# Gather, running sum and product: 64 gather slots in place of 16, at most 8 gathers on their way, a new order of sums and products

## The chip, the cores and the metric

The kernel runs on one core of a Trainium2 chip. The metric is the device time of one execution in microseconds (us); where runs are timed, it is the median of several. A run counts as slow when it takes over 1.5% more than the fastest run of the same kernel. The time of an execution is 1.7 to 1.8 us longer than the span of its profile, so spans are compared with spans and times with times.

## The reference

```python
B, S, N, D = (16, 4096, 2048, 512)
gathered = x[b_idx, indices, :].copy()   # 2048 sorted rows of 4096, for each of 16 batches
cs = np.cumsum(gathered, axis=1)         # running sum over the rows
return np.matmul(cs, w)                  # w is 512 x 512, all fp32
```

The kernel cuts this into 256 tiles of 128 rows. A tile's gather reads 128 rows of 2,048 bytes from HBM, the chip's memory, and writes them as fp16; a tile's result is 128 rows of 2,048 bytes in fp32.

## The kernel before

Five engines and the queue of stores work as a pipeline. They wait for each other on semaphores, which are counters (`need`, `then_inc`). A slot is the buffer that takes the gathered rows of one tile. **POOL** issues one indirect DMA a tile, which gathers the rows and casts them on the way:

```python
def gather(t):
    g, r = divmod(t, R)                       # R = 2 tiles make a pair
    pool.need(s_a, R * (g + 1) - NG)          # PE has summed the tile that had this slot (NG = 16)
    ...                                       # which column of indices
    nc.gpsimd.indirect_dma_start(
        out=g16[g % (NG // R)][:, r, :], ...
    ).then_inc(s_g[t % NG], 16)
```

**PE** multiplies the tile by a triangle of ones, which gives running sums inside the tile, already transposed (`sums`); **DVE** adds the last column of the tile before (`carry`); PE multiplies by `w` (`project`); **ACT** copies the product to an output buffer; SP stores four tiles (1 MB) at a time:

```python
def sums(t, u, first=None):
    pe.need(s_g[t % NG], 16 * (t // NG + 1), tiles)     # gather t has landed
    ...                                                 # four matmuls, 128 x 128 each
def project(u, t, first=None):
    ...
    pe.need(s_d, ...)                                   # DVE has done the carry
    ...                                                 # four matmuls, 128 x 512 each
```

PE runs its instructions in order, and the order is fixed beforehand: sums run some tiles ahead of products.

```python
for u in range(T):
    lead = min(LEAD, 1 + (u + 2) // 4, 1 + (T - 1 - u) // 6)    # LEAD = 4
    first = u if u // R in PLAIN else u // R * R + R - 1
    while done < T and done <= max(first, u + lead):
        order.append((True, done))       # sums of tile `done`
        done += 1
    order.append((False, u))             # product of tile u
```

## Time and profile before

Before the prediction the kernel took 354.54 us (median of 3 runs, 354.28 to 355.03). The execution that was profiled was a slower one: it took 355.99 us, with a span of 354.3 us.

Three periods compete in the middle of the run: POOL's for issuing a gather, PE's for computing a tile, and that of the DMA engines for moving one. Ask which is the longest; the prediction works them out, and shows the lines. None of the engines' shares alone says so: PE is counted busy for 86% of the span, 304.4 us, which is 25 us more than 256 tiles take where nothing holds it.

### The profile page before, as it was taken

The page shows a single profiled execution, that of the slowest core. Times are in us where ns is not written, and L with a number is a line of the kernel's source. Part 1 is how long each engine was busy: PE and PEld are TensorE (multiplying, and loading weights), DVE is VectorE, ACT ScalarE, POOL GpSimd, SP SyncE. Part 2 cuts the span into 40 slices and gives each one's busy share as a digit, 9 for nine tenths or more (in the row PEclk, how much of TensorE's full clock was granted, in tenths as well). Part 3 has the DMA queues.
Part 4 walks back from the last instruction along what each step waited for, and adds up shares of the span by engine and source line. Part 5 has one row for each costly group of instructions (what it writes and reads, how often), then busy time and mean ns, then how long its engine had stood idle before and what let it go on. Part 6 is the DMA issues. An engine that isn't in the chain of part 4 may idle for free.

```text
span 354.3 us, 6077 instructions
## 1 busy us (share of the span) xinstructions
PE 304.4 (86%) x2066; PEld 152.7 (43%) x2066; DVE 179.2 (51%) x263; ACT 152.4 (43%) x260; POOL 241.9 (68%) x266
## 2 busy tenths in 40 slices
PE   7787969889888898988889898888989889899993
PEld 2343525444444453444444344444445444444441
DVE  2563635545555554555555455455545546455441
ACT  2242525434444443443444344453444444344542
POOL 6777777777777777777777777776776767676000
PEclk9998989999999999999999999999999999999998
DMA  7999999999999999999999999999999999999995
GB/s 190 170 221 256 256 297 262 304 296 283 320 290 298 311 297 298 303 309 282 306 315 285 301 306 303 286 319 301 285 312 300 301 296 306 302 290 317 301 328 228
DMA packets 56010, 102.12 MB, mean 288 GB/s; under 512 B 5824, under 2 KB 38848, under 8 KB 56000
## 3 DMA queue, kind: packets, MB, share of 16 engines
q0 software_dynamic: 36864, 33.57, 58.9%
q1 hardware_dynamic: 18576, 67.90, 50.0%
q10 hardware_dynamic: 560, 0.53, 0.6%
q8 instruction: 5, 0.08, 0.1%
q14 instruction: 5, 0.04, 0.0%
HBM read 68.42 MB, written 67.11 MB: 383 GB/s over the span
## 4 chain that ended last, share of the span: by engine, by line
DMA 58%; POOL 20%; PE 12%; issue 8%; POOLq 0%; ACT 0%; SPq 0%
DMA g<-in_x_dram,idxg 58%; POOL g L120 20%; PE pb L183 9%; PE pa L139 4%; DMA idx_first<-in_indices_dram 1%; POOLq L279 0%; ACT ob L195 0%; SPq L403 0%; SPq L88 0%
## 5 line engine op out<-in xcount | busy, mean ns | idle before, releaser
L120 POOL DMA_INDIRECT g<-in_x_dram,idxg x252 | 236.4, 938 | 82.2 <-issue 64.2
L183 PE MATMUL pb<-w,cst 128*128 128x512 f16 x1024 | 264.8, 382 | 1.4 <-DVE cst L171 1.0
L171 DVE TENSOR_TENSOR cst<-pa,cst 128x512 f16<-128x512 f32 x240 | 166.1, 692 | 152.9 <-PE pa L139 151.5
L195 ACT COPY ob<-pb 128x512 f32<-128x512 f32 x256 | 149.8, 585 | 191.8 <-PE pb L183 191.8
L139 PE MATMUL pa<-ut,g 128*128 128x128 f16 x1008 | 99.5, 222 | 40.7 <-DMA g<-in_x_dram,idxg 39.5
L139 PEld LDWEIGHTS pa<-ut,g 128*128 128x128 f16 x1008 | 70.1, 98 | 124.0 <-DMA g<-in_x_dram,idxg 90.9
L183 PEld LDWEIGHTS pb<-w,cst 128*128 128x128 f16 x1024 | 89.9, 98 | 64.6 <-issue 2.5
L158 DVE CAST cst<-pa 128x512 f16<-128x512 f32 x16 | 11.1, 692 | 9.4 <-PE pa L139 9.4
L285 PE MATMUL pb<-zeros 128*128 128x512 f16 x16 | 5.7, 519 | 1.5 <-DVE zeros L289 1.5
L120 POOL DMA_INDIRECT g<-in_x_dram,idx_first x4 | 3.9, 986 | 1.6 <-issue 0.9
L285 PEld LDWEIGHTS pb<-zeros 128*128 128x128 f16 x16 | 1.9, 125 | 4.0 <-issue 2.0
L292 DVE CAST idxf<-idx 128x128 f32<-128x128 uint32 x2 | 0.5, 227 | 4.5 <-DMA idx<-in_indices_dram 4.5
L358 ACT ACT_TABLE_LOAD x1 | 1.3, 1283 | 2.5 <-issue 2.5
L361 ACT CAST w<-w 128x512 f16<-128x512 f32 x2 | 1.1, 614 | 2.8 <-DMA w<-in_w_dram 2.8
L139 PE MATMUL pa<-uq,g 128*128 128x128 f16 x16 | 1.6, 220 | 0.2
L139 PEld LDWEIGHTS pa<-uq,g 128*128 128x128 f16 x16 | 1.0, 97 | 1.6 <-DMA g<-in_x_dram,idxg 0.6
L297 PE MATMUL pb<-ident,idxf 128*128 128x128 f32 x2 | 0.7, 374 | 0.7 <-DVE idxf L292 0.7
L297 PEld LDWEIGHTS pb<-ident,idxf 128*128 128x128 f32 x2 | 0.4, 183 | 1.6 <-DVE idxf L292 1.3
L306 DVE CAST w<-w 128x512 f16<-128x512 f32 x2 | 0.8, 445 | 0.4 <-DMA w<-in_w_dram 0.4
L289 DVE MEMSET zeros<- 128x256 uint32 x1 | 0.3, 272 | 1.1 <-SPq L88 1.1
L303 DVE CAST idxg<-pb 128x128 uint32<-128x128 f32 x2 | 0.6, 288 | 0.2 <-PE pb L297 0.2
L245 POOL MEMSET ident<- 128x128 f32 x1 | 0.2, 204 | 0.5 <-SPq L88 0.5
(10 smaller groups left out, 1.9 us busy)
## 6 DMA issues: line engine op xcount, KB each, us to landing
out_dram<-ob SPq DMA_DIRECT2D x62, 1024.0 KB, 8.0
g<-in_x_dram,idxg POOLq DMA_INDIRECT x252, 15.7
out_dram<-ob SPq DMA_DIRECT2D x4, 256.0 KB, 3.2
out_dram<-ob SPq DMA_DIRECT2D x2, 512.0 KB, 4.2
w<-in_w_dram ACTq DMA_DIRECT2D x2, 256.0 KB, 3.9
w<-in_w_dram SPq DMA_DIRECT2D x2, 256.0 KB, 4.4
idx<-in_indices_dram SPq DMA_DIRECT2D x2, 128.0 KB, 3.1
g<-in_x_dram,idx_first POOLq DMA_INDIRECT x4, 4.0
```

The lines of the kernel that those rows point to most:

```text
L120: nc.gpsimd.indirect_dma_start(out=g16[g % (NG // R)][:, r, :], out_offset=None, in_=x_flat, in_offset=bass.IndirectOffsetOnAxis(ap=ap, ax ...
L139: mm = nc.tensor.matmul(out=pa[t % NA][:, c], lhsT=g16[g % (NG // R)][:, r, c * P : (c + 1) * P], rhs=uq[:] if first is None and g in PLAI ...
L158: nc.vector.tensor_copy(out=dst, in_=src).then_inc(s_d, 1)
L171: nc.vector.tensor_tensor(out=dst, in0=src, in1=last, op=mybir.AluOpType.add).then_inc(s_d, 1)
L183: mm = nc.tensor.matmul(out=pb[u % NB][:], lhsT=cst[g % NC][:, c, j, :], rhs=w16[:, c, :], start=(c == 0), stop=(c == DC - 1),)
L195: nc.scalar.copy(out=ob[g // W % NO][:, g % W, j], in_=pb[u % NB][:]).then_inc(s_e, 1)
L285: nc.tensor.matmul(out=pb[NB - 1][:], lhsT=zeros[:, :P], rhs=zeros[:], start=True, stop=True)
L297: nc.tensor.transpose(out=pb[k % NB][:, :P], in_=idxf[:, k, :], identity=ident[:]).then_inc(s_pt, 1)
L303: nc.vector.tensor_copy(out=idxg[:, k, :], in_=pb[k % NB][:, :P]).then_inc(s_prep, 1)
L306: nc.vector.tensor_copy(out=w16[:, c, :], in_=w32[:, c, :]).then_inc(s_wc, 1)
L358: nc.scalar.copy(out=spare[:], in_=zeros[:, :1])
L361: nc.scalar.copy(out=w16[:, c, :], in_=w32[:, c, :]).then_inc(s_wc, 1)
```

## The change

The intent is to uncouple the gathers from PE (64 slots), to keep the DMA queue short (8 on their way), and to start products sooner at the beginning and sums sooner at the end. The core of the diff:

```diff
-    NG = 16
+    NG = 64
+    FLY = 8
+    NS = 32
+    FREE = 8
...
+    V = NG
...
-        pool.need(s_a, R * (g + 1) - NG)
+        if t % FREE == 0:
+            pool.need(s_a, t + FREE - NG)
+        if t >= FLY:
+            pool.need(s_g[(t - FLY) % NS], 16 * ((t - FLY) // NS + 1))
...
-        lead = min(LEAD, 1 + (u + 2) // 4, 1 + (T - 1 - u) // 6)
+        lead = min(LEAD, 1 if u < 2 else 2 + (u + 4) // 12, (T - 1 - u) // 2)
...
-    step = 2 * U
+    step = 2 * V
...
-    with nc.tensor.Fori(2 * U // R, (T - 2 * U) // R, U // R) as first:
+    with nc.tensor.Fori(2 * U // R, (T - 2 * U) // R, V // R) as first:
```

The rest counts semaphores relative to the loop's start, since a round of PE's loop now has 64 tiles.

More of the change, by code (lines that the diff above doesn't have):

```diff
@@ L62 @@
     U = NT
-    assert U % NG == 0 and U % (W * R * NO) == 0 and U % NA == 0 and U % (R * NC) == 0 and U % NB == 0
+    V = NG
+    assert V % NS == 0 and NS == 16 * R and 2 * U % NS == 0 and (T - 4 * U) % V == 0 and U % (W * R * NO) == 0 and U % NA == 0 and U % (R * NC) == 0 and U % NB == 0
     assert D == 512 and N % (R * P) == 0 and T % P == 0
@@ L99 @@
     s_ol = sem("s_ol")
-    s_g = [sem(f"s_g{i}") for i in range(NG)]
+    s_g = [sem(f"s_g{i}") for i in range(NS)]
     s_o = [sem(f"s_o{i}") for i in range(NO)]
@@ L125, in gather @@
             element_offset=(t // NT) * S * D,
-        ).then_inc(s_g[t % NG], 16)
+        ).then_inc(s_g[t % NS], 16)
     PLAIN = (0, G - 1)
@@ L133, in sums @@
         tiles = None if first is None else R * first
-        pe.need(s_g[t % NG], 16 * (t // NG + 1), tiles)
-        pe.need(s_d, t - NA + 1, tiles)
+        skip = 0 if first is None else 2 * U
+        pe.need(s_g[t % NS], 16 * (t // NS + 1) - skip // R, first)
+        pe.need(s_d, t - NA + 1 - skip, tiles)
         for c in range(DC):
             if c == 1 and u is not None:
-                pe.need(s_e, u - NB + 1, tiles)
+                pe.need(s_e, u - NB + 1 - skip, tiles)
             mm = nc.tensor.matmul(
@@ L141, in sums @@
                 lhsT=g16[g % (NG // R)][:, r, c * P : (c + 1) * P],
-                rhs=uq[:] if first is None and g in PLAIN else ut[:],
+                rhs=uq[:] if g in PLAIN else ut[:],
                 start=(c == 0),
@@ L177, in project @@
         tiles = None if first is None else R * first
-        pe.need(s_e, u - NB + 1, tiles)
-        pe.need(s_d, u + 1 if first is None and g in PLAIN else R * (g + 1), tiles)
+        skip = 0 if first is None else 2 * U
+        pe.need(s_e, u - NB + 1 - skip, tiles)
+        pe.need(s_d, (u + 1 if g in PLAIN else R * (g + 1)) - skip, tiles)
         for c in range(DC):
             if c == 2 and t is not None:
-                pe.need(s_d, t - NA + 1, tiles)
+                pe.need(s_d, t - NA + 1 - skip, tiles)
             mm = nc.tensor.matmul(
@@ L330 @@
     tail = order.index((False, T - 2 * U - 1)) + 1
-    step = 2 * U
+    step = 2 * V
     for i in range(head + step, tail):
-        assert order[i] == (order[i - step][0], order[i - step][1] + U)
+        assert order[i] == (order[i - step][0], order[i - step][1] + V)
     def run(i, first=None):
@@ L337, in run @@
         after = next((v for k, v in order[i + 1 :] if k != is_sums), None)
-        if first is not None:
-            t -= 2 * U
-            after -= 2 * U
         if is_sums:
```

## The prediction

> **What bounds the kernel now.** I read the page first, then the DMA view for single stretches, then the chain of work that ended last and POOL's waits.
>
> From the page of the kernel before:
>
> ```profile
> PE 304.4 (86%) x2066; PEld 152.7 (43%) x2066; DVE 179.2 (51%) x263; ACT 152.4 (43%) x260; POOL 241.9 (68%) x266
> ...
> q0 software_dynamic: 36864, 33.57, 58.9%
> q1 hardware_dynamic: 18576, 67.90, 50.0%
> ...
> L120 POOL DMA_INDIRECT g<-in_x_dram,idxg x252 | 236.4, 938 | 82.2 <-issue 64.2
> ...
> g<-in_x_dram,idxg POOLq DMA_INDIRECT x252, 15.7
> ```
>
> Queue 0 carries the gathers (counted as the fp16 bytes that are written), queue 1 mostly the stores. Their packets together take 109% of what 16 engines have: some overlap, and little room. PE's 86% is no proof of a PE bound: where nothing holds it, the timeline shows a tile every 1.09 us (sums at 22.46 and 23.55 us), which is 279 us for 256 tiles, and PE's waits show 39.5 us for gathers. POOL could be the bound: between two gathers lie 938 ns of work and 0.30 us of "issue", 1.24 us a tile, 318 us in all.
>
> The DMA view of the long middle (75 to 325 us), of a microsecond with gathers alone (307 to 308), and of two with stores alone (345 to 347) decide it:
>
> ```profile
> DMA packets 40650, 75.01 MB, mean 300 GB/s; under 512 B 3850, under 2 KB 28509, under 8 KB 40648
> ...
> DMA packets 228, 0.20 MB, mean 203 GB/s; under 512 B 30, under 2 KB 228, under 8 KB 228
> ...
> DMA packets 208, 0.82 MB, mean 408 GB/s; under 512 B 6, under 2 KB 10, under 8 KB 208
> ```
>
> A tile's gather writes 128 x 512 fp16 = 131,072 bytes: at 203 GB/s, 0.646 us. A tile's store is 262,144 bytes: at 408 GB/s, 0.643 us. One after the other that is 1.29 us, and the middle really needs 393,216 bytes / 300 GB/s = **1.31 us a tile**. So the two simply share the 16 engines in time, and the engines have no free time from 75 us on. 1.31 is above POOL's 1.24 and PE's 1.09. 256 tiles x 1.31 = 335 us; the span is 354.3. The other 19 us are engine time lost at the two ends. Of the first 25 us, gathers (2.08 MB at 203 GB/s) use 10.2 and queue 1 (1.88 MB) and the weights' queue (0.53 MB) at 408 GB/s use 5.9, so 9 are lost; from 25 to 50 us (2.34 and 4.45 MB) 2.6 are lost; from 340 us to the end (0.07 and 3.76 MB) 4.8.
>
> The end, in the chain from 320 us, and POOL's waits from 200 to 320 us:
>
> ```profile
> 325.73 20.86 DMA g<-in_x_dram,idxg
> 346.59 0.05 issue
> 346.63 0.40 PE pa L139 x4
> 347.03 0.86 PE pb L183 x4
> 347.89 0.01 issue
> 347.90 1.04 PE pb L183 x4
> 348.94 0.02 issue
> 348.96 0.59 ACT ob L195
> ...
> POOL g L120 <- issue: 21.8, 71, 0.5
> POOL g L120 <- PE pa L139: 11.9, 22, 1.1
> ```
>
> The last gather is issued at 325.7 and lands 20.9 us later. Counting gathers between issue and landing in the trace gives 2 on their way in the first 20 us, 7 at 60 to 80 us, 15 from 200 us on. POOL runs at 1.24 us against 1.31 for the engines, so the queue grows until 16 slots are full at about 200 us; from then POOL waits for PE. This wait is a symptom: it costs nothing, because gathers lie ready on the engines all the time.
>
> Each gather is counted in by 16 engines. In the trace's semaphore records 13 of the 16 arrive within about 2 to 4 us, and the last three up to 6 to 9 us after the first (gather 255: first 338.1, median 339.4, last 346.6 us). So a few engines are slower, and the slowest sets when a tile is there.
>
> **What the Trainium skill says.** "DMA: Bandwidth & Descriptors", section "Issuing engines are not separate DMA queues": DMAs started from any engine end on the same 16 and interleave. The trace agrees: 1.29 us worked out against 1.31 measured. The same page, "Where 436 GB/s comes from", puts the ports' ceiling at 435 GB/s; stores alone reached 408, and gathers alone 203 written, which is 406 read since each element shrinks from four bytes to two. So both run close to that ceiling, and a rearrangement of waits has some 7% to win at the very most. The same page, "Latency and other measured facts", says that engines 7 and 15 are usually slower, with a guess that the rings of software descriptors are the cause; the trace has a few late engines in every gather, but does not name them.
>
> **The change part by part.**
>
> 1. *64 slots.* They let gathers run up to 64 tiles ahead of PE. They can be filled only if tiles land faster than PE eats them. Tiles land every 1.31 us, PE needs 1.09: they stay empty. What they remove is POOL's wait for PE, 18.0 us in the whole run, which covered a full queue. Worth 0 us on the end.
>
> 2. *At most 8 on their way.* This is the part that binds. From some 60 us on POOL will wait for the gather eight before. Does the queue of the slowest engine ever run dry? When gather t-8 has landed, seven remain: 7 x 1.31 = 9.2 us of work; the new one needs 1.24 us for POOL and, from the first gathers (issued until 4.31, landed at 8.07), 3.8 us to land. 9.2 covers 5.0. The kernel before moved 291 GB/s at 60 to 80 us, with 7 on their way, against 300 in the middle, and part of those 3% is the mix there. So 0 to +3 us. Against that, fast engines can no longer run 7 us (5 tiles) ahead of the slow ones. If the slow ones are slow because the fast ones crowd them, this evens them out: the median engine finished the last gather 7 us before the slowest, so perhaps -4 us; if they are slow by themselves, 0. I give the first one chance in three: -1.3 us. Landing time should fall to about 8 x 1.31 = 10.5 us less POOL's own time, from 15.7; that shortens no path, as the engines stay full.
>
> 3. *More waits on POOL.* One on a gather's semaphore per gather, one on PE per 8 (before: one on PE per pair). Before, gathers with and without a wait had the same 1.24 us period, so a wait already met hides under the 938 ns. 0 us.
>
> 4. *Order at the start.* Writing both orders out: sums lead by 2 and 3 where they led by 3 and 4, up to tile 19. Stores begin about one tile earlier where the engines are underused: one tile's store is 0.64 us. -0.7 us.
>
> 5. *Order at the end.* The lead stays 4 until tile 247, then falls to 0; only product 255 is left behind the last sums, where two were. In the chain that removes 0.86 us of PE, but the carry on DVE (0.69 us) then stands open in front of the product, and products 247 and 251 come one sums later. -0.1 us, with a spread of 1.
>
> 6. *PE loop of 64 tiles in place of 16.* Three rounds in place of twelve. PE stood 2.5 us in "issue" before products, and it has 0.2 us a tile to catch up in. 0 us.
>
> Sum: 354.5 + 1 - 1.3 - 0.7 - 0.1 = 353.4; I lean slightly lower, as a shallower queue may also disturb the stores less, and take **352.5 us**.
>
> **The rivals.** *A: the cap takes the place of the slots and starves the engines.* For it: the late engines use up most of the eight, so that fast ones hold only 2 or 3, and gathers alone drain at 0.65 us while POOL supplies one in 1.24. Against: the slow engine sets the end, and has seven. If it bites, a tile goes to 1.34 or 1.36 us: 362 to 367 us. *B: the cap evens out the engines.* For it: the spread of 6 to 9 us appears only as the queue grows (about 1.5 us in the first 40 us). Against: it could grow simply because slow engines fall behind. Time 348 to 350 us. *C: POOL becomes the bound*, each wait costing 0.1 us: 1.34 us a tile, 360 us. Against it: the equal periods above. *D: products are held up by late gathers, and 64 slots cure it.* PE does wait, but for data, not for slots; then nothing is gained.
>
> **Range and chances.** The engines' 335 us stay. What moves is inside the 19 us at the ends, and I see at most 5 of them won. Low 347.5 (B with the gain at the start), high 358 (a mild A). Faster than 2% means below 347.5: 0.11. Slower than 2% means above 361.6, A or C in full: 0.07. Within: 0.82.
>
> **What would show each step.** Right: the middle still at about 300 GB/s; landing time about 9 us; POOL's waits for PE gone and in their place waits for gathers, from 60 us on; a last gather issued some 10 us later (about 336 us) and landing at 344 to 347; PE still waiting for gathers. A shows as the middle below 295 GB/s; B as 16 arrivals closer together and the last landing before 343; C as a POOL period over 1.3 us in the first 40 us. I am wrong if the engines move more than 305 GB/s in the middle: then queue depth itself cost throughput, and nothing in this trace says so.

## The result, and the profile after

The changed kernel took **354.76 us** (median of 4 runs, 354.56 to 355.15) beside 354.78 us of the kernel before. Ratios here are the mean time of one kernel's fast runs over that of the other's of the same rounds, so not quite the ratio of the medians; this one is 1.0001, with a 95% interval of 0.9983 to 1.0019. A second set of runs gave 1.0000 (0.9980 to 1.0021). The forecast of 2 us less did not come.

The page of the changed kernel, in the lines that answer to those of before:

```profile
PE 302.0 (85%) x2066; PEld 151.1 (43%) x2066; DVE 179.3 (51%) x263; ACT 152.4 (43%) x260; POOL 242.0 (68%) x266
...
q0 software_dynamic: 36864, 33.57, 59.2%
q1 hardware_dynamic: 18576, 67.90, 49.7%
...
L127 POOL DMA_INDIRECT g<-in_x_dram,idxg x252 | 236.5, 939 | 89.9 <-issue 55.1
...
g<-in_x_dram,idxg POOLq DMA_INDIRECT x252, 9.3
```

One number moved: the median gather lands 9.3 us after its issue in place of 15.7. Everything that costs time stayed. A shorter stay in a queue is no shorter run, when the server behind the queue is as busy as before. That it is, the DMA view of 75 to 325 us shows:

```profile
DMA packets 40624, 75.36 MB, mean 301 GB/s; under 512 B 3836, under 2 KB 28379, under 8 KB 40619
```

301 GB/s where it was 300: 393,216 bytes / 301 = 1.31 us a tile, as before. POOL's waits in the whole run (total us, times, longest):

```profile
POOL g L127 <- issue: 56.0, 177, 1.4
POOL g L127 <- DMA g<-in_x_dram,idxg: 29.9, 62, 1.1
POOL g L127 <- PE pa L147: 4.9, 16, 0.3
```

The wait for PE fell from 18.0 us (42 times) to 4.9, and a wait for gathers of 29.9 us took its place. Each of these times holds the 0.30 us that lie between any two gathers, so 16 waits that make 4.9 us are no wait at all. Without this gap there were some 5 us of waiting before (18.0 - 42 x 0.30) and some 11 us now (29.9 - 62 x 0.30). POOL has time to spare; a run below takes these waits away, and the time stays.

The chain of work that ended last, from 335 us:

```profile
328.59 9.62 DMA g<-in_x_dram,idxg
338.21 0.05 issue
338.26 0.40 PE pa L147 x4
338.66 1.73 PE pb L192 x8
340.38 0.22 PE pa L147 x4
340.61 1.73 PE pb L192 x8
...
346.58 0.24 PE pa L147 x4
346.82 0.02 issue
346.84 0.70 DVE cst L179
347.55 0.05 issue
347.59 1.05 PE pb L192 x4
348.64 0.02 issue
348.67 0.58 ACT ob L204
```

Here is what looks like a gain and is none. The last gather now lands at 343.4 us (344.1 in the second profile) and not at 346.6. But PE no longer waits for it: from 338.26 us on it does nine products, some of them held behind sums until then, and five sums, with one gap of 0.77 us for the last carry on DVE. Its last product ends at 348.64 where it was 348.94. From the last landing to the end of the span there are now 10.0 us (10.6 in the second profile); before there were 7.7.

### The profile page after: what moved, and what is told of

Same layout as the page of the kernel before. It is cut to its first block, busy times and chain, and to the rows that moved or that the text cites. A ratio compares the mean times of both kernels' runs of the same rounds, so it can differ in the third digit from the quotient of the medians.

```text
span 353.4 us, 6043 instructions
## 1 busy us (share of the span) xinstructions
PE 302.0 (85%) x2066; PEld 151.1 (43%) x2066; DVE 179.3 (51%) x263; ACT 152.4 (43%) x260; POOL 242.0 (68%) x266
## 4 chain that ended last, share of the span: by engine, by line
DMA 54%; POOL 27%; issue 10%; PE 6%; DVE 0%; ACT 0%; POOLq 0%; SPq 0%
DMA g<-in_x_dram,idxg 54%; POOL g L127 27%; PE pb L192 5%; PE pa L147 2%; DMA idx_first<-in_indices_dram 1%; DVE cst L179 0%; ACT ob L204 0%; POOLq L26 0%; SPq L409 0%; SPq L92 0%
## 5 line engine op out<-in xcount | busy, mean ns | idle before, releaser
L147 PE MATMUL pa<-ut,g 128*128 128x128 f16 x1008 | 98.5, 220 | 42.5 <-DMA g<-in_x_dram,idxg 41.6
L147 PEld LDWEIGHTS pa<-ut,g 128*128 128x128 f16 x1008 | 68.9, 98 | 126.0 <-DMA g<-in_x_dram,idxg 92.9
```

The costliest lines, as they stand in the source:

```text
L147: mm = nc.tensor.matmul(out=pa[t % NA][:, c], lhsT=g16[g % (NG // R)][:, r, c * P : (c + 1) * P], rhs=uq[:] if g in PLAIN else ut[:], star ...
```

## The experiments

The first explanation (theory 1) was that the cap had really won 3 us at the last landing, and that the new order at the end gave them back. Four kernels take the change apart.

**The cap alone**, on the kernel before:

```diff
+    FLY = 8
...
+        if t >= FLY:
+            pool.need(s_g[(t - FLY) % NG], 16 * ((t - FLY) // NG + 1))
```

> The kernel before with one thing added: a gather waits until the one eight before it has landed (16 slots, order and PE loop as before). Theory 1 (the cap wins some 3 us at the last landing, and the new order at the end gives them back): 352 to 353.3 us, last landing near 343, at least 1.3 us faster than before. Theory 2 (the cap is neutral on the landing path, the earlier landing of the profiled run is chance): 354.3 to 355.2 us, last landing near 346.

Measured: 355.35 us, ratio 1.0020 (1.0002 to 1.0039). The last landing is at 345.8 us, the landing time:

```profile
g<-in_x_dram,idxg POOLq DMA_INDIRECT x252, 9.0
```

So the cap alone brings the whole fall of the landing time, and it buys nothing; if anything it costs some 0.7 us (0.1 to 1.4). The chain that ended last shows why an earlier last landing would by itself have bought nothing:

```profile
327.37 11.10 DMA g<-in_x_dram,idxg
338.47 0.05 issue
338.51 0.40 PE pa L142 x4
338.91 0.86 PE pb L186 x4
```

It leaves the gathers at 338.47 us, 7 us before the last one lands, and stays with PE and the last carry until the last copy. Theory 1 falls.

**The new order alone**, on the kernel before, with 16 slots and no cap:

```diff
-        lead = min(LEAD, 1 + (u + 2) // 4, 1 + (T - 1 - u) // 6)
+        lead = min(LEAD, 1 if u < 2 else 2 + (u + 4) // 12, (T - 1 - u) // 2)
```

> The kernel before with the new order of sums and products alone. Theory 1: the new start wins 0.7 us, the end loses 1 to 2 us because at most of the last ten tiles four products still stand behind late sums: 355 to 356.2 us. Theory 2 (order is neutral or a win, as predicted): 353.7 to 354.6 us.

Measured: 355.14 us, ratio 1.0012 (0.9991 to 1.0034). That is in theory 1's range and not in theory 2's, but the interval holds both, and the cap alone has refuted the other half of theory 1. The last gather lands at 343.6 us, although there is no cap. So the earlier landing belongs to the order and not to the cap. From it to the end of the span there are 9.9 us.

**The changed kernel with the old order** at both ends, and **with the old order at the end alone**:

```diff
-        lead = min(LEAD, 1 if u < 2 else 2 + (u + 4) // 12, (T - 1 - u) // 2)
+        lead = min(LEAD, 1 + (u + 2) // 4, 1 + (T - 1 - u) // 6)                      # both ends
+        lead = min(LEAD, 1 if u < 2 else 2 + (u + 4) // 12, 1 + (T - 1 - u) // 6)     # end alone
```

> The changed kernel with the order of before at both ends. Theory 1: equal to the cap alone within 0.5 us, so 352 to 353.3 us (64 slots and the loop of 64 are worth nothing). Theory 2: 354.5 to 355.5 us.

> The changed kernel with its own start, and at the end the leads of before. Theory 1: the best of the four, about 0.7 us under the one with the old order at both ends, 351.5 to 352.8 us; last landing near 343, and the last product some 2 us sooner than in the changed kernel (347 us in the profile in place of 348.6). Theory 2: 353.7 to 354.8 us.

Measured: 354.69 us, ratio 1.0004 (0.9987 to 1.0022), and 354.77 us, ratio 1.0007 (0.9987 to 1.0027). Neither won what theory 1 expected. Last landings: 345.6 and 345.0 us, with 8.6 and 8.1 us from there to the end of the span. The new theory (E) says that the 16 DMA engines have a fixed amount of work and hardly any free time between some 50 and 340 us. Whatever lands gathers sooner would then let stores go later, and the reverse. This last part is argued: the stores still to go after 340 us are 3.4 to 3.8 MB in the four profiles with the new order at both ends, and 3.3 to 3.8 in the four with the old order at the end and a lead of 4.

Three runs test it, and one more asks about the order.

**Half the stores**, on the kernel before:

```diff
-            out=rows.rearrange("(g p j) d -> p g j d", p=P, j=R),
-            in_=src[:, g % W : g % W + n],
+            out=rows.rearrange("(g p j) d -> p g j d", p=P, j=R)[:, :, 0:1],
+            in_=src[:, g % W : g % W + n, 0:1],
```

> The kernel before, storing only one row of each pair in all but the first and last two tiles of pairs; the output is wrong on purpose. Theory E (the 16 DMA engines bound the middle, 0.646 us a gather plus 0.643 us a store): a tile now needs some 0.97 us of the engines, POOL's 1.24 us becomes the bound, 3 + 318 + 5 to land + 8 = 334 us (330 to 338). Rival F (a wait or queue outside the engines, such as slots, POOL or PE, sets 1.31 us a tile): 351 us or more.

Measured: 337.18 us, ratio 0.9508 (0.9473 to 0.9543). Its DMA view of 75 to 325 us, then its gathers' landing time:

```profile
DMA packets 42797, 53.11 MB, mean 212 GB/s; under 512 B 4030, under 2 KB 29753, under 8 KB 42794
```

```profile
g<-in_x_dram,idxg POOLq DMA_INDIRECT x252, 5.2
```

A tile now moves 262,144 bytes: at 212 GB/s, 1.24 us, which is POOL's period and no longer the engines'. No slot, wait or order was touched, and the time fell by 17 us, to where the next limit stands. The landing time fell to 5.2 us by itself, because the queue is gone. This is what a relief of the real bound looks like. Output buffers that come free sooner are no rival: the page of the kernel before puts all of ACT's idle time before its copies, 191.8 us, down to PE and none to a store. What the run does not separate is the 16 engines from the memory behind them, whose load fell as well; "the engines" stands here for both.

**At most 4 on their way**, and **at most 32**, on the changed kernel (`FLY = 4`, `FLY = 32`):

> The changed kernel with at most 4 gathers on their way. A loaded gather took 9.3 us in the changed kernel, some 5 us unloaded with POOL's own time. Theory E: the engines are no longer kept full, a tile takes 6 to 6.5 us / 4 = 1.5 to 1.6 us, so 395 to 425 us. Rival G (queue depth is irrelevant down to a few): 354 to 358 us.

> The changed kernel with up to 32 on their way. Theory E: engine time is the same at any depth that keeps them full; POOL then runs at 1.24 us a tile without a wait, some 15 to 17 are on their way at the end as the queue grows by one in 25 us: 354 to 355.5 us. Rival H (a deep queue hurts, which is what the cap is for): over 357 us. Rival I (the slots' wait did cost): under 352.5 us.

With 4: 417.47 us, ratio 1.1741 (1.1682 to 1.1801), within what theory E expected. The DMA view of 75 to 325 us and POOL's longest wait:

```profile
DMA packets 33541, 62.09 MB, mean 248 GB/s; under 512 B 3174, under 2 KB 23475, under 8 KB 33535
```

```profile
POOL g L127 <- DMA g<-in_x_dram,idxg: 68.4, 64, 3.4
```

The landing time is 5.2 us, the shortest of the comparable kernels with full stores, and the time is the longest: less is moved, 248 GB/s. With 32: 354.93 us, ratio 1.0013 (0.9978 to 1.0048). POOL's waits there:

```profile
POOL g L127 <- issue: 75.6, 248, 0.3
POOL g L127 <- PE pa L147: 2.1, 7, 0.3
```

POOL never waits any more: what is left is the gap of 0.3 us. The gathers on their way grow to 14 on average at 240 to 260 us and 16 at 300 to 320 us, never over 18. POOL's wait for slots is gone, and the time is the same. That wait was a symptom.

**Sums at most 2 tiles ahead**, on the kernel before (`LEAD = 2`):

> The kernel before with sums that lead products by at most 2 tiles in place of 4. Theory J (stores that come two tiles sooner move 1.3 us of engine time from the end, where PE at 1.09 us a tile cannot feed stores of 0.64 us, to the start, where engines are idle): 353.0 to 354.0 us. Rival K (PE then stands on the carry of DVE and loses): over 355.5 us. Within 0.3% of before: order is no lever at all.

Measured: 354.38 us, ratio 0.9988 (0.9961 to 1.0015): within 0.3%, no lever that can be seen.

The next three runs, a cap of 6, the changed kernel with half the stores, and small stores at both ends, ran on a chip on which the kernel before took 405.63 us.

> The changed kernel with at most 6 on their way. With 4, a tile took 417 / 256 = 1.6 us, so a loaded gather came back about 6.4 us after its wait ended; full engines need 1.31 us a tile, which 6 on their way give as long as a gather comes back within 7.9 us. If depth matters only below what keeps the engines full, a slight loss: 355 to 362 us. If the cap of 8 already costs a good part, 6 gives over 365 us.

> The changed kernel with the stores halved, wrong on purpose, against the kernel before with the stores halved (337.2 us). There POOL's issue of 1.24 us a tile is the bound. If the added waits on POOL are hidden, 336.5 to 338 us; if each gather's wait cost 0.1 us, 360 us.

> The kernel before with what the engines' lost time at the ends asks for: sums lead by at most 2, the first six and last four pairs of tiles are stored one pair at a time. Some 1 to 2 us of store work move to the start and the end's queue is fed sooner: 352.5 to 353.9 us, 0.2 to 0.6% under before. If the ends can't be shortened by earlier stores: 354.2 to 355.2 us.

Measured there: 465.29, 465.44 and 408.63 us. They answer nothing of what was asked, for something else held the kernels there. The profile of the first shows it in its waits from 25 to 75 us:

```profile
ACT ob L204 <- remote: 35.3, 2, 21.8
DVE cst L179 <- remote: 27.4, 2, 19.6
DVE cst L179 <- issue: 21.7, 1, 21.7
```

DVE and ACT stood still for some 20 us at a time, waiting for something that the profile does not show, while POOL went on issuing gathers. The two kernels with 64 slots were 14% slower there than the kernel before. What this was stays open; none of it is used below. The three were run again elsewhere, with the changed kernel as a control.

> The changed kernel as it is, as a control. On a chip where the kernel before takes 354 to 355 us: 354 to 355.5 us. On a chip like the one of the last three runs, where the kernel before took 405.6 us: some 465 us, if the 64 slots are what made the two derived kernels slow there, or about 406 us if it was the smaller store or the cap of 6.

> The same as the run with at most 6 on their way, again: its chip had the kernel before at 405.6 us, so it said nothing of the question. On a chip with the kernel before at 354 to 355 us: 355 to 362 us if depth matters only below what keeps the engines full, over 365 us if the cap of 8 already costs a good part.

> The changed kernel with halved stores again, wrong on purpose. Against 337.2 us of the kernel before with halved stores: 336.5 to 338 us if POOL's added waits are hidden, 360 us if each cost 0.1 us.

> The kernel before with sums leading by at most 2 and stores one pair at a time at both ends, again: 352.5 to 353.9 us if earlier stores shorten the ends, 354.2 to 355.2 us if they cannot.

Measured: the control 355.05 us (the ratio of 1.0000 above). **At most 6**: 361.71 us (median of four runs, of which the slow one is left out of the ratio), ratio 1.0178 (1.0136 to 1.0220), with 295 GB/s in the middle. So 8 is the first of the depths tried that keeps the engines full. **Half the stores on the changed kernel**: 338.61 us, ratio 0.9538 (0.9519 to 0.9558), against 0.9508 for the same on the kernel before. The intervals overlap, but all four runs (338.15 to 338.87) lie above those of the kernel before with half the stores (336.59 to 337.81), and above what was expected. POOL's added waits are not the cause: the last gather is issued at the same time in both profiles, so they cost nothing where POOL is the bound. The kernel before with half the stores, then the changed one:

```profile
320.60 0.94 POOL L120 DMA_INDIRECT g<-in_x_dram,idxg  x1 [0.30 <-issue]
```

```profile
320.64 0.94 POOL L127 DMA_INDIRECT g<-in_x_dram,idxg  x1 [0.30 <-issue]
```

The 1.9 us between the spans (337.2 and 335.3) arise later. Once the chain has left the gathers, at 319.8 and 320.9 us, PE has eleven products left in the changed kernel and eight in the other. That points to the new order at the end; no run tests it there. **Small stores at both ends**, on the kernel before:

```diff
-    LEAD = 4
+    LEAD = 2
...
-    for g in range(W):                 # pairs stored one at a time
+    for g in range(3 * W):
...
-    for g in range(G - W, G):
+    for g in range(G - 2 * W, G):
```

(The semaphores of these extra stores are counted accordingly.) Measured: 354.20 us, ratio 0.9980 (0.9962 to 0.9998). It is the only full version whose interval lies below 1, by 0.2%, at the edge of what can be told from nothing, and where "cannot" was expected to begin.

## Why the prediction was right or wrong

**Right: the bound.** The prediction called the engines' shared time the bound, at 1.29 us a tile against 1.31 measured, and POOL's wait a symptom. Halving the stores, and depths of 4, 6 and 32, confirm it. "Perfetto Trace Analysis" in the Trainium skill, section "What 'DMA-bound' means", separates DMA engines from the sequencer that issues, POOL here, as possible bounds. The runs show both, one after the other: the engines at full stores, POOL's 1.24 us at half stores.

**Right: the moved wait.** It expected landing after about 9 us (9.3), POOL's waits for PE replaced by waits for gathers, the middle at 300 GB/s (301), no cost of slots, loop and POOL's waits. The last gather was issued at 333.6 us, where about 336 was expected, and landed at 343.4, just before the 344 to 347 expected. Two readings were rough: the 18.0 us of POOL's waits hold the ordinary gaps, and a recount gives 14 gathers on their way after 200 us, on average, where the prediction has 15.

**Wrong: the sum.** The forecast of 2.0 us less was made of five terms: +1 for a mild loss by the cap, -1.3 for engines that even out, -0.7 and -0.1 for the order at the two ends, and a lean of -0.9. The runs gave +0.7 us (0.1 to 1.4) for the cap alone, +0.4 (-0.3 to +1.2) for the order alone, and 0.0 (-0.6 to +0.7) for the whole. None of the four gains can be seen.

**Wrong: engines that even out (-1.3 us, part 2, rival B).** Of its two signs, closer arrivals came, and a last landing before 343 us did not. Over tiles 100 to 239, the median time from a gather's first to its last of 16 arrivals fell from 7.2 us to 4.6 in the changed kernel, and to 4.0 with the cap alone. But a cap that holds back the engines that are ahead narrows this time by itself. That the late ones became faster is not shown: the middle went from 300 to 301 GB/s, and the cap alone was 0.2% slower. The step that failed is the path: it took an earlier last landing for a shorter run. It had read this from one profile, the only one in which the chain ends with the last landing. In the nine other profiles of kernels that store everything and have a cap of 8, of 32 or none (the one odd chip left out), the chain leaves the gathers at 336.3 to 339.6 us and goes on over PE, which still has seven to ten products to do, and the last carry. The last landing is not on it. Nor do even arrivals bring an early last landing: with the order alone the arrivals are 9.7 us apart, and the last landing is at 343.6 us; with the cap alone they are 4.0 us apart, and it is at 345.8.

The landings themselves follow the order. With the new order at both ends it came at 343.1 to 344.1 us, under a cap of 8, under a cap of 32 and with 16 slots and no cap. With the old order at the end and a lead of 4 it came at 345.0 to 346.6 us, with and without the cap. (With a lead of 2, it came at 343.7 and 344.2 us.) The span then went on for 9.9 to 10.6 us in the first group and for 7.7 to 8.6 in the second. Every one of these eight spans lies between 353.0 and 354.7 us.

**Wrong: the lean of 0.9 us** "as a shallower queue may also disturb the stores less". Landing of a 1 MB store took 8.0 us before and 7.9 after. Nothing supported this term, and it was almost half of the forecast.

**Not confirmed: the start (-0.7 us, part 4).** The first half of the step came. With the order alone, queue 1 moved 6.68 MB in the first 50 us in place of 6.33, which at 408 GB/s is 0.9 us. At the prediction's rates all queues together used 38.6 us of engine time before and 39.2 in the changed kernel, there through gathers (4.57 MB in place of 4.42). But the order alone did not shorten the run: its interval reaches from -0.3 to +1.2 us. Where the time was lost again is not shown. At the same rates, the engines' lost time after 325 us is 5.0 us in the kernel before and with the order alone, and 5.1 in the changed kernel, so these profiles do not show it at the end.

**Wrong: the order at the end (-0.1 us, part 5).** It left out the products that are held behind sums until the last gathers: PE has nine of them to do from 338.26 us on. At full stores this made no difference that can be seen; with half the stores the changed kernel's span is 1.9 us longer, which points to this order, but was not tested alone.

How the remaining tenths of a microsecond divide between the start, the end and the cap's small cost cannot be told with runs that scatter by 2 us.

So, apart from the lean, the wrong terms had the same fault. A gain in one part was booked as a gain of the whole, without asking what would set the end once that part was sooner.

## What to carry to other kernels

When a shared resource is full, work out its total work and its idle time, and ask of each change which of the two it lowers; landing times, waits and queue depths can all improve without either falling. A cap on transfers in flight needs to be just deep enough to keep the engines fed: here 4 cost 17%, 6 cost 1.8%, and 8 and 32 were within 0.2%. And a sum of small expected gains that lies below the scatter of the runs is better forecast as no change.

## What the Trainium skill lacked or had wrong

- "DMA: Bandwidth & Descriptors" has no rate for a gather that casts. Here 128 rows of 2 KB, cast from fp32 to fp16, wrote 203 GB/s alone (406 GB/s read), and stores in pieces of at most 4 KB ran at 408 GB/s; the two shared the engines in time, 1.29 us worked out against 1.31 measured. The page's ceiling of 435 GB/s ("Where 436 GB/s comes from") was not reached in these stretches.
- No page says how many software-issued gathers must be on their way to keep the engines full. Here, beside stores: 248 GB/s with 4, 295 with 6, 301 with 8, and 301 with 32 allowed.
- "DMA: Bandwidth & Descriptors", "Latency and other measured facts", calls engines 7 and 15 usually slower and gives a guess why. Here the last of 16 arrivals came 7.2 us after the first (median) with 16 slots and 4.6 in the changed kernel. These records do not name the engine, so neither the numbers 7 and 15 nor the guess is shown.
- No page was found to cover the behaviour of the one chip where the kernel before took 405.63 us and DVE and ACT stood still for up to 21.8 us at a time.
